# VectorE and ScalarE take over GpSimd's products in a hybrid decoder block, and the S5 response copies are queued later

## The chip, the cores and the metric

One core of one Trainium2 chip runs one launch of the kernel. The metric is device time in microseconds (us) of that core, the median of several executions. Engines are named as the profile names them: PE is TensorE (PEld its weight loads), DVE is VectorE, ACT is ScalarE, POOL is GpSimd, SP is the sync engine, whose queue issues the DMAs (q in a name, as in SPq, is an engine's own queue).

## The reference

One decoder layer for 1024 tokens of width 1024 in float32: a mixer of four gated delta-rule heads beside 32 groups of a complex diagonal state space (S5), then attention to 256 memory tokens, then a SwiGLU, and a last RMSNorm. Cut to what the change touches:

```
q, k, v = silu(causal_conv4(rmsnorm(h) @ w_in))          # 4 heads of 128
g  = -exp(a_log) * softplus(a + dt_bias); beta = sigmoid(b)
o  = gated_delta_rule(l2norm(q), l2norm(k), v, g, beta)  # in chunks
o  = o * rsqrt(mean(o*o) + EPS) * norm_g * silu(z)
x_t = ab * x_{t-1} + bb u_t   (complex)                  # S5, 64 states a group
y  = gelu(Re(C x_t) + D u_t)
y  = y * sigmoid(y @ w_glu + b_glu)
h += concat(o, y) @ w_out
h += cross_attn(rmsnorm(h), rmsnorm(mem)) @ w_xo
h += (silu(n(h) @ w_gate) * (n(h) @ w_up)) @ w_down      # n: rmsnorm
out = rmsnorm(h) * norm_final_g
```

## The kernel before, in words

Every matrix product is made of three matmuls: each operand is split into a high part (ScalarE's copy, L62) and a low part (a subtraction, L63, on VectorE or GpSimd as the caller says), and `mm3` (L79 to L81) adds high x high, low x high and high x low in PSUM. The activations are kept transposed, 128 features by 512 tokens a tile.

The stages follow each other: input norm; S5 set-up, whose four rounds of `s5_pre` leave each group's response in DRAM (TD), from which `s5_toeplitz` copies the tile TT, eight DMAs of 256 KB each from DRAM to DRAM; the gates (`gates`, L525 to L560: decay g, its running sums gc and gr, beta); the memory's norm (`mem_prep`, L804 to L826); four heads, each with its input products, a convolution (L489 to L492), `dn_a` (from L566, which reads gr back through DRAM, gD, into the broadcast tile d_Qg, and takes from it the chunk decays dn_al and d_kdc), `dn_v` and `dn_b`; then, interleaved, the recurrence over chunks (`dn_seq`, `dn_tail`), S5 (`s5_in`, `s5_out`) and the memory's key and value products; `glu`; the out-projection; attention; the SwiGLU's first half; the down products; and `final`.

`s5_out` (L378 to L418) makes, for each pair of groups, complex products of real parts: for real and imaginary part a first product z1 on VectorE (L392, L405), a second product z2 (L393 and L406 on GpSimd, names s_m), their sum or difference (L394, L409), and between the two halves a scan along the tokens (L398, s_S). There are 8 calls with 2 products of each kind in each half, so 32 second products. `dn_tail` (L780 to L800) takes a chunk's output po from PSUM, sums its squares on ScalarE (L791), makes an rsqrt of 11 small VectorE operations (L85 to L89, d_ro), multiplies po by it (L795, VectorE) and by the gate sz (L796, GpSimd), and lets TensorE transpose (L799).

The down products run in five blocks of four activation tiles. `down_acts` loads the block's eight 128x512 tiles, makes differences of them (L1255) and splits them; `down_weights` splits four pairs of weight tiles a block, one of each pair on VectorE (128x1024, whi and wlo from wraw) and one on GpSimd (128x768, from wb); `down_products` adds seven PSUM results a row tile to hT or Q (L1325, VectorE). The last tiles of the SwiGLU's first half are summed at L1197 (VectorE) and multiplied at L1204 (GpSimd) just ahead of it.

PSUM pools: pm has three banks (name mm), p5 one (name aux; the convolutions, the gates and the memory norm use it), p6 one; `final` runs with pa's five.

The order of instructions on each engine isn't the program's: a scheduler in the framework, which simulates a timeline, sets it when the kernel is built; a wait on an engine's queue holds up everything behind it. `issue_after` makes an instruction come no sooner in that order than the one named.

## Time and profile before

| | us |
|---|---|
| median of 3 runs | 1603.62 (1600.15 to 1607.66) |
| profiled execution, its own time | 1605.2 |
| its span | 1603.2 |
| PE busy | 1457.7 (91%) |
| VectorE busy | 1188.9 (74%) |
| GpSimd busy | 655.9 (41%) |
| ScalarE busy | 634.7 (40%) |

The mean granted TensorE clock is 0.958 of full speed. The span is what the trace covers; the profiled execution's own time is 2.0 us longer. A row of a timeline reads: start, duration, engine, line, operation, output and inputs, and in brackets how long the engine stood idle before it and what released it. A row with "x4" is four instructions in a run. A row of a stretch gives the stretch, its length, busy time and instructions (x) of PE, PEld, DVE, ACT and POOL, the granted clock, the share of DMA time and GB/s.

### The profile page before, as it was taken

How to read it: one execution, taken by the hardware profiler on the slowest of the kernel's cores; microseconds unless marked ns; L12 is line 12 of the kernel's file. 1: busy time of each engine (PE TensorE's matmuls, PEld its weight loads, DVE VectorE, ACT ScalarE, POOL GpSimd, SP SyncE). 2: the span in 40 equal slices, each digit the busy share in tenths (PEclk: the TensorE clock that was granted, in tenths of full speed). 3: DMA queues.
4: the chain of work that ended last, by engine and by line, in shares of the span. 5: the costliest groups of instructions: out<-in, count | busy, mean ns of one | idle time of the engine just before them, and what ended most of it. 6: DMA issues, size and time to landing. Idle time of an engine off the chain costs nothing.

```text
span 1603.2 us, 20926 instructions
## 1 busy us (share of the span) xinstructions
PE 1457.7 (91%) x7326; PEld 1218.8 (76%) x7326; DVE 1188.9 (74%) x2164; ACT 634.7 (40%) x1137; POOL 655.9 (41%) x475
## 2 busy tenths in 40 slices
PE   6887699996978788999999999999999998999985
PEld 4787488886877576878888788888888886777864
DVE  8969489886699797775546697666666668899886
ACT  5222353452544563454443442333333334533322
POOL 6175234324552416620010443333333347766544
PEclk9999899997989988999999999999999999999997
DMA  7256454548688152245524414444444357444302
GB/s 224 80 164 199 134 133 124 140 119 293 213 291 265 47 197 105 79 131 171 171 92 165 144 33 145 149 142 139 145 137 137 112 168 251 149 146 150 126 10 105
DMA packets 146616, 237.49 MB, mean 148 GB/s; under 512 B 12464, under 2 KB 79440, under 8 KB 143952
## 3 DMA queue, kind: packets, MB, share of 16 engines
q1 hardware_dynamic: 146512, 236.17, 45.7%
q8 instruction: 57, 0.93, 0.2%
q14 instruction: 47, 0.39, 0.1%
HBM read 169.69 MB, written 68.53 MB: 149 GB/s over the span
## 4 chain that ended last, share of the span: by engine, by line
PE 53%; DVE 24%; DMA 9%; issue 5%; ACT 4%; POOL 3%; SPq 1%; DVEq 0%; POOLq 0%; ACTq 0%
PE aux L81 9%; PE aux L79 9%; PE aux L80 9%; PE mm L81 8%; PE mm L79 8%; PE mm L80 8%; DVE aux L491 2%; DVE wlo L63 1%; DVE d_R L675 1%; DMA s_wb<-in_s5bT 1%; DVE s_S L398 1%; POOL wlo L63 1%; DVE hT L1380 1%; DMA d_R<-LD 1%; DMA wraw<-in_w_xk 1%
## 5 line engine op out<-in xcount | busy, mean ns | idle before, releaser
L62 ACT ACTIVATE whi<-wraw 128x1024 fp32r<-128x1024 f32 (+2 forms) x152 | 139.7, 922 | 202.3 <-PE mm L80 67.3
L79 PE MATMUL mm<-AH,whi 128*128 128x512 f32 x448 | 178.4, 399 | 1.4 <-DVE hT L1325 1.4
L81 PE MATMUL mm<-AH,wlo 128*128 128x512 f32 x432 | 170.9, 396 | 0.0
L80 PE MATMUL mm<-AL,whi 128*128 128x512 f32 x408 | 161.3, 396 | 0.0
L150 POOL TENSOR_TENSOR acc<-acc,sq 128x512 f32<-128x512 f32 (+1 forms) x41 | 53.1, 1295 | 212.9 <-ACT sq L149 212.1
L63 DVE TENSOR_TENSOR wlo<-wraw,whi 128x1024 fp32r<-128x1024 f32 (+1 forms) x76 | 97.9, 1290 | 33.2 <-ACT whi L62 33.1
L1204 POOL TENSOR_TENSOR sg<-sg,ca 128x512 f32<-128x512 f32 x40 | 58.2, 1456 | 144.1 <-DVE sg L1197 92.7
L63 POOL TENSOR_TENSOR wlo<-wraw,whi 128x1024 fp32r<-128x1024 f32 x28 | 67.8, 2422 | 115.8 <-ACT whi L62 98.8
L79 PEld LDWEIGHTS mm<-AH,whi 128*128 128x128 f32 x448 | 84.6, 189 | 20.9 <-DVE hT L1325 2.9
L81 PEld LDWEIGHTS mm<-AH,wlo 128*128 128x128 f32 x432 | 81.5, 189 | 18.3 <-issue 0.4
L80 PEld LDWEIGHTS mm<-AL,whi 128*128 128x128 f32 x408 | 77.1, 189 | 16.6
L80 PE MATMUL aux<-AL,whi 128*128 128x512 f32 x216 | 85.0, 393 | 0.7 <-POOL AL L63 0.7
L79 PE MATMUL aux<-AH,whi 128*128 128x512 f32 x176 | 69.7, 396 | 0.0
L62 ACT ACTIVATE wlo<-graw 128x512 fp32r<-128x512 f32 x62 | 38.8, 626 | 62.7 <-PE aux L81 53.1
L81 PE MATMUL aux<-AH,wlo 128*128 128x512 f32 x160 | 63.4, 396 | 0.0
L491 DVE SCALAR_TENSOR_TENSOR aux<-pre,convw,aux 128x512 f32<-128x512 f32 x72 | 54.1, 751 | 8.3 <-ACT aux L489 7.5
L1202 ACT ACTIVATE ca<-ca 128x512 f32<-128x512 f32 x40 | 25.3, 633 | 83.5 <-DVE ca L1197 83.0
L63 POOL TENSOR_TENSOR wlo<-wb,whi 128x768 fp32r<-128x768 f32 x19 | 39.8, 2094 | 42.3 <-ACT whi L62 42.3
L81 PE MATMUL aux<-AH,whi 128*128 128x512 f32 x136 | 53.4, 392 | 0.0
L80 PEld LDWEIGHTS aux<-AL,whi 128*128 128x128 f32 x216 | 40.6, 188 | 10.6 <-POOL AL L63 1.4
L63 DVE TENSOR_TENSOR wlo<-graw,wlo 128x512 fp32r<-128x512 f32 x40 | 46.0, 1150 | 2.2 <-ACT wlo L62 2.2
L79 PE MATMUL aux<-AH,wlo 128*128 128x512 f32 x120 | 47.3, 394 | 0.0
(713 smaller groups left out, 4678.2 us busy)
## 6 DMA issues: line engine op xcount, KB each, us to landing
graw<-in_w_up SPq DMA_DIRECT2D x22, 512.0 KB
acc<-in_w_down SPq DMA_DIRECT2D x42, 256.0 KB
actD<-sg SPq DMA_DIRECT2D x40, 256.0 KB
WD<-acc SPq DMA_DIRECT2D x40, 256.0 KB
wraw<-in_w_in SPq DMA_DIRECT2D x16, 512.0 KB
d_X<-XD SPq DMA_DIRECT2D x8, 1024.0 KB
wraw<-AD SPq DMA_DIRECT2D x16, 512.0 KB
wraw<-VD SPq DMA_DIRECT2D x16, 512.0 KB
```

Of the source, the lines that this page charges most:

```text
L62: self.a.activation(out=hi, in_=src, func=AF.Copy)
L63: return (eng or self.v).tensor_tensor(out=lo, in0=src, in1=hi.bitcast(F32), op=ALU.subtract)
L79: mm(ps, wh, xh, start=first, stop=False)
L80: mm(ps, wh, xl, start=False, stop=False)
L81: mm(ps, wl, xh, start=False, stop=last)
L150: eng.tensor_tensor(out=acc, in0=acc, in1=tmp, op=ALU.add)
L398: v.tensor_tensor_scan(out=Zs[:, k, q], data0=self.m8[:, 2 * b + q:2 * b + q + 1].to_broadcast([P, P]), data1=Z[:, k, q], initial=0.0, op0 ...
L491: v.scalar_tensor_tensor(out=acc, in0=pre[:, 1 + i:1 + i + HT], scalar=cw(i), in1=acc, op0=ALU.mult, op1=ALU.add)
L675: tt(out=R[:, i, :, 0:i], in0=R[:, i, :, 0:i], in1=X[:, :, 0:i], op=ALU.mult)
L1202: A.activation(out=r, in_=r, func=AF.Silu)
L1204: g.tensor_tensor(out=r, in0=r, in1=sg[o], op=ALU.mult)
L1380: self.v.scalar_tensor_tensor(out=dst, in0=dst, scalar=self.gain(4, m), in1=rb, op0=ALU.mult, op1=ALU.mult)
```

## The change

It has eight parts.

1. `s5_out`: the 32 second products are made by VectorE.
2. `gates` and `mem_prep`: their PSUM tiles come from pm (three banks) and no longer from p5 (one).
3. `dn_a`: dn_al and d_kdc are copied by ScalarE instead of VectorE.
4. `dn_tail`: VectorE multiplies po by sz, and four ScalarE copies scale the quarters by ro.
5. `glu`: the sigmoid is written in place in PSUM, and VectorE multiplies from there, eight times, instead of GpSimd.
6. `down_acts`: all splits and differences are VectorE's; ten operations a block of the down products move from GpSimd.
7. `final`: the broadcast row sums are read from PSUM by VectorE; ScalarE's copy of them serves only GpSimd, which multiplies three of the eight row tiles (m = 1, 3, 5) and no longer four.
8. `s5_toeplitz` is called after the first head's `dn_a`, behind that head's load of d_Qg.

```
@@ s5_out (L393, L406)
-            g.tensor_tensor(out=z2, in0=ri, in1=Pv[:, 1 - k], op=ALU.mult)
+            tt(out=z2, in0=ri, in1=Pv[:, 1 - k], op=ALU.mult)
...
-            g.tensor_tensor(out=z2[:, :, N], in0=ri[:, :, N], in1=Zs[:, 1 - k, :, N], op=ALU.mult)
+            tt(out=z2[:, :, N], in0=ri[:, :, N], in1=Zs[:, 1 - k, :, N], op=ALU.mult)
@@ gates, twice (L551, L557); mem_prep alike (L817)
-        ps = self.p5.tile([P, HT], F32, name="aux")
+        ps = self.pm.tile([P, HT], F32, name="mm")
@@ dn_a (L582, L588, L589)
-        self.load(Qg, self.gD.rearrange("(c h) p -> h c p", h=4)[hd:hd + 1].to_broadcast(sh))
+        self.first = self.load(Qg, self.gD.rearrange("(c h) p -> h c p", h=4)[hd:hd + 1].to_broadcast(sh))
...
-        v.tensor_copy(out=al, in_=Qg[:, :, P - 1])
-        v.tensor_copy(out=kdc, in_=E[:, :, P - 1])
+        A.activation(out=al, in_=Qg[:, :, P - 1], func=AF.Copy)
+        A.activation(out=kdc, in_=E[:, :, P - 1], func=AF.Copy)
@@ dn_tail (L795, L796)
-        v.tensor_tensor(out=on, in0=po, in1=ro.unsqueeze(2).to_broadcast(sh), op=ALU.mult)
-        g.tensor_tensor(out=on, in0=on, in1=sz, op=ALU.mult)
+        v.tensor_tensor(out=on, in0=po, in1=sz, op=ALU.mult)
+        for i in range(4):
+            A.activation(out=on[:, i], in_=on[:, i], func=AF.Copy, scale=ro[:, i:i + 1])
@@ glu (L908 to L911)
-                self.a.activation(out=sg, in_=ps, func=AF.Sigmoid, bias=self.bglu[:, m:m + 1])
+                self.a.activation(out=ps, in_=ps, func=AF.Sigmoid, bias=self.bglu[:, m:m + 1])
...
-                self.g.tensor_tensor(out=yy, in0=yy, in1=sg, op=ALU.mult)
+                self.v.tensor_tensor(out=yy, in0=yy, in1=ps, op=ALU.mult)
@@ down_acts (L1233); its put(...) and sub(...) calls on self.g become g
-        v, g = self.v, self.g
+        v = g = self.v
@@ final (L1373 to L1380)
+        ps = self.pa.tile([P, HT], F32, name="aux")
+        self.row_sums(rs, n // P, ps)
         rb = self.tmp.tile([P, HT], F32, name="res", bufs=2)[:, 0:n]
-        self.rowbc(rs, n // P, rb)
+        self.a.activation(out=rb, in_=ps[:, 0:n], func=AF.Copy)
...
-            if m % 2 == 1:
+            if m in (1, 3, 5):
                 self.g.tensor_tensor(out=dst, in0=dst, in1=rb, op=ALU.mult)
+            elif m == 7:
+                self.v.tensor_tensor(out=dst, in0=dst, in1=ps[:, 0:n], op=ALU.mult)
             else:
-                self.v.scalar_tensor_tensor(out=dst, in0=dst, scalar=self.gain(4, m), in1=rb, op0=ALU.mult, op1=ALU.mult)
+                self.v.scalar_tensor_tensor(out=dst, in0=dst, scalar=self.gain(4, m), in1=ps[:, 0:n], op0=ALU.mult, op1=ALU.mult)
@@ the stages
-                self.s5_toeplitz(S)
...
                         B = self.dn_a(hd, q, k, dp, dx)
+                        if hd == 0:
+                            with self.tc.issue_after(self.first.ins):
+                                self.s5_toeplitz(S)
```

Lines below L550 or so move by one in the changed kernel (L595 stays, L821 becomes L822, L1197 becomes L1198, L1255 becomes L1256).

The scheduler orders the instructions anew. On PE, ahead of the first head's k and q norms, the last small sums stood behind nearly all input products (L79 to L81); L552 and L558 are the gates' sums, L120 and L821 the memory norm's column and row sums, L595 the transposes of the first head's tile `it`. Before:

```order
L821 MATMUL aux<-cst,rsm 128x128 x2
L79 MATMUL mm<-AH,whi 128x512
L80 MATMUL mm<-AL,whi 128x512
L81 MATMUL mm<-AH,wlo 128x512
L595 MATMUL da<-cst,it 128x128 x4
```

After, from the last of the S5 set-up's matmuls (L334):

```order
L334 MATMUL aux<-s_G,s_bb 32x128 x7
L552 MATMUL mm<-gt_g,cst 128x32
L558 MATMUL mm<-cst,gt_g 32x128
L120 MATMUL mm<-ones,acc_1642 128x64 x2
L822 MATMUL mm<-cst,rsm 128x128 x2
L79 MATMUL mm<-AH,whi 128x512
```

All four small sums now stand in one run ahead of 96 products, and L595 (eight at once) follows those.

On SP's queue, in the same place; gr is the running sum's row form, gD its copy in DRAM, wraw the weights to come, kD the finished k. Before:

```order
L54 DMA TD<-s_Ks 16x4x128 x2
L54 DMA TT<-TD 512x128
L54 DMA SD<-s_W_1073 128x2x512
L54 DMA TT<-TD 512x128 x7
L54 DMA gD<-gr 32x128
L54 DMA wraw<-in_w_in 128x1024
L54 DMA d_Qg<-gD 128x8x128
```

After:

```order
L54 DMA TD<-s_Ks 16x4x128 x2
L54 DMA gD<-gr 32x128
L54 DMA wraw<-in_w_in 128x1024 x2
L54 DMA SD<-s_W_1073 128x2x512
L54 DMA d_Qg<-gD 128x8x128
L54 DMA TT<-TD 512x128 x8
L54 DMA kD<-it 128x1024
```

The eight TT copies now stand behind gD and d_Qg, and ahead of kD.

On VectorE, at the last sums of the SwiGLU's first half (ca and sg are its results) and the first operands of the down products (AH, AL). Before:

```order
L1197 TENSOR_TENSOR ca<-res,mm 128x512
L1255 TENSOR_TENSOR AH<-AH 128x512
L1197 TENSOR_TENSOR sg<-res,mm 128x512
L1290 TENSOR_TENSOR acc_11296<-acc_11296 128x256
L1255 TENSOR_TENSOR AH<-AH 128x512
L1291 TENSOR_TENSOR acc_11296<-acc_11295,acc_11296 128x256
L1255 TENSOR_TENSOR AH<-AH 128x512
L1292 TENSOR_TENSOR acc_11295<-acc_11296,acc_11295 128x256
L1197 TENSOR_TENSOR ca<-fsg,aux 128x512
L1293 TENSOR_TENSOR acc_11295<-acc_11295 128x256
L1255 TENSOR_TENSOR AH<-AH 128x512 x2
L1197 TENSOR_TENSOR sg<-fsg,aux 128x512
```

After:

```order
L1198 TENSOR_TENSOR ca<-res,mm 128x512
L1256 TENSOR_TENSOR AH<-AH 128x512 x2
L1198 TENSOR_TENSOR sg<-res,mm 128x512
L1291 TENSOR_TENSOR acc_11312<-acc_11312 128x256
L1256 TENSOR_TENSOR AH<-AH 128x512 x2
L1292 TENSOR_TENSOR acc_11312<-acc_11311,acc_11312 128x256
L1198 TENSOR_TENSOR ca<-fsg,aux 128x512
L1256 TENSOR_TENSOR AH<-AH 128x512 x2
L1293 TENSOR_TENSOR acc_11311<-acc_11312,acc_11311 128x256
L63 TENSOR_TENSOR AL<-AH,AL 128x512 x2
L1198 TENSOR_TENSOR sg<-fsg,aux 128x512
```

More differences and two splits of the first down block stand ahead of the last sg.

14 lines of the change are left out of this document (7 added, 7 removed).

## The prediction

> **What bounds the kernel now.** I read the page first, then the busy time of each engine by stage, then the waits and the timeline wherever TensorE stands still. The profiled execution took 1605.2 us, 1603.2 of it span and 2.0 around it; the median of the runs shown, 1603.62, lies 1.6 below it. About 0.5% or 8 us is what a measurement of this kernel can tell from no change.
>
> ```profile
> PE 1457.7 (91%) x7326; PEld 1218.8 (76%) x7326; DVE 1188.9 (74%) x2164; ACT 634.7 (40%) x1137; POOL 655.9 (41%) x475
> ```
>
> TensorE is busy 91% of the span, so nothing that merely relieves VectorE (DVE) or GpSimd (POOL) counts by itself. What counts are the 145 us in which PE is idle. The busy time by stretch shows where they are; columns are PE, PEld, DVE, ACT, POOL, then the granted TensorE clock, the DMA share and GB/s.
>
> ```profile
> 180.00:190.00 10.00, 1.32 (x8) 0.82 (x6) 1.21 (x4) 3.14 (x4) 4.22 (x2) 0.76 0.20 56
> 190.00:200.00 10.00, 4.03 (x14) 3.42 (x15) 9.54 (x19) 6.51 (x10) 4.99 (x4) 0.56 0.15 50
> 370.00:380.00 10.00, 1.85 (x13) 1.69 (x13) 4.34 (x14) 1.80 (x3) 2.01 (x1) 0.65 0.97 303
> 440.00:520.00 80.00, 64.29 (x475) 61.13 (x476) 73.03 (x179) 38.72 (x99) 31.46 (x29) 0.91 0.84 281
> 550.00:560.00 10.00, 1.26 (x5) 0.86 (x5) 6.85 (x13) 1.95 (x3) 2.61 (x2) 0.69 0.23 82
> 1409.00:1448.00 39.00, 38.68 (x167) 31.07 (x166) 37.42 (x45) 15.88 (x23) 25.16 (x14) 1.00 0.46 148
> ```
>
> PE stands still or goes short in the stretch ahead of the first head (180 to 197), at the memory weights (370), in the S5 states (440 to 520) and at the last delta-rule tail (550); two more such places, the start of the down products and the final norm, have their rows below. The change touches all but 370 directly. In the down products themselves (1409) PE is full and VectorE nearly so: 38.68 and 37.42 of 39.
>
> **The change part by part.**
>
> *The gate and memory sums on other PSUM buffers, al and kdc on ScalarE, the TT copies later.* A row of the waits, then VectorE, SP and PE in order of time:
>
> ```profile
> DVE dn_al L588 <- ACT d_Qg L586: 13.7, 1, 13.7
> 158.96 0.35 DVE L550 RECIPROCAL beta<-gt_e 128x32 f32<-128x32 f32 x1
> ...
> 169.47 5.57 SPq L54 DMA_DIRECT2D TT<-TD  x7
> 172.99 0.16 DVE L129 TENSOR_SCALAR rs_ms<-aux 128x2 f32<-128x2 f32 x1 [4.50 <-PE aux L120]
> 174.96 0.16 DVE L89 SCALAR_TENSOR_TENSOR rsm<-rs_w,rsm 128x2 f32<-128x2 f32 x1
> 175.14 0.62 SPq L54 DMA_DIRECT2D gD<-gr  x1
> ...
> 192.97 2.32 DVE L491 SCALAR_TENSOR_TENSOR aux<-pre,convw,aux 128x512 f32<-128x512 f32 x3
> ...
> 195.97 1.12 PE L595 MATMUL da<-cst,it 128*128 128x128 f32 x4 [14.66 <-ACT it L492]
> ```
>
> VectorE waits 13.7 us at L588 for the chain gD, d_Qg, E, Exp, and the convolution (L491) is queued behind it; PE waits 14.7 us for that. In the new order VectorE has no L588, the sums run ahead of the 96 input products and gD leaves before TT. PE then waits earlier, at the memory norm (L822 right behind L120): VectorE is busy with the gates' sigmoid until L550 ends at 159.3, the norm's small operations take 2.1 (172.99 to 175.12), so the last L822 falls near 161.7, and 96 products at 38.68/167 = 0.232 us end near 184. Before, 24 products more were done ahead of L595, which came at 195.97 and took 1.1. With these 24 (5.6 us) and L595's eight now together (2.0), PE has at 191.6 the work that it had at 197.1: -5.5 us. Bounds: -10 (of the 14.7 only the early wait of some 5 is left) to -2 (the early wait grows to 12, when VectorE takes the S5 tables first). The granted clock of 0.56 behind the idle stretch is a part of that loss. A sentence apart: the Trainium skill, "TensorE: Matmul & The Clock Gate", Part 1, has the clock halved after an idle window of about 3.4 us until about 3.4 us of work have passed; by it each long pause closed saves a further estimated 1.7 us, which would make the three PE pauses here, at 181, 549 and 1338, worth 5 us more than I put down; the rows agree that the clock falls.
>
> In the four heads PE is otherwise full; the same L588 waits fall away there, and ScalarE, 40% busy, takes 8 small copies. I put -1 with the memory weights at 370, where DMA is 97% busy and the eight 256 KB TT copies now lie nearer: -4 to +4.
>
> *S5 second products on VectorE.* Min, median and max in ns of the scan, who waits for it, of half of what moves (L406), and the scan at its worst with the GpSimd operation of that moment:
>
> ```profile
> L398 DVE TENSOR_TENSOR_SCAN s_S<-s_m,s_Z x32: 392/411/2587, 385.0 to 492.0; 128x128 f32<-128x128 f32 x32
>   POOL s_m L406: 18.2, 8
> L406 POOL TENSOR_TENSOR s_m<-s_M,s_S x16: 712/762/1253, 387.0 to 493.3; 128x254 f32<-128x254 f32 x16
> 455.05 2.50 DVE L398 TENSOR_TENSOR_SCAN s_S<-s_m,s_Z 128x128 f32<-128x128 f32 x1
> 454.74 2.53 POOL L63 TENSOR_TENSOR wlo<-wraw,whi 128x1024 fp32r<-128x1024 f32 x1
> ```
>
> The same scan takes 0.41 alone and 2.50 when it lies under a GpSimd operation of 2.53. The 32 products cost VectorE 32 x 0.42 = 13.4. They take 32 x 0.76 = 24 us from GpSimd; if VectorE was held in half of it, 12 come back, and the two sides nearly cancel. What remains is handing over: GpSimd waits 18.2 for the scan, eight times, and VectorE in turn for s_m; for these eight round trips I count 0.6 each, which leaves -4 with rounding (13.4 - 12 - 5), since VectorE (73 of 80) is the bound there. Bounds: -10 (half of the 18.2 on the chain) and +4 (only a quarter of the 24 had held VectorE: 13.4 - 6 - 4). A sentence apart: the Trainium skill, "SBUF — State Buffer", section "SBUF: two separate sides", says that of the two engines whoever starts first holds the shared ports for its whole instruction; the 2.50 agrees with it, and by it all 24 could come back, so the term would be an estimated -14.
>
> *End of the delta rule and the GLU.*
>
> ```profile
> 545.30 0.28 ACT L791 ACTIVATE d_R<-po 128x128 f32<-128x128 f32 x1 [3.09 <-PE po L777]
> 552.15 0.69 DVE L795 TENSOR_TENSOR d_R<-po,d_ro 128x512 f32<-128x512 f32 x1
> 552.97 1.59 POOL L796 TENSOR_TENSOR d_R<-d_R,d_L 128x512 f32<-128x512 f32 x1 [1.95 <-issue]
> 554.62 1.11 PE L799 MATMUL po<-cst,d_R 128*128 128x128 f32 x4 [6.15 <-POOL d_R L796]
> 555.86 1.74 SPq L54 DMA_DIRECT2D kst<-memD  x4
> 559.85 0.58 PE L79 MATMUL mm<-kvh,whi 128*128 128x256 f32 x1 [4.12 <-ACT kvh L62]
> ```
>
> From L795 to L799 stand 2.47 us; afterwards four ScalarE scales of a 128x128 quarter stand there (0.28 each by L791, 1.1 together) and the product with sz is off the chain: -1.4. The kst load, which comes when all of this is done, and the K product behind it move along. The GLU's eight products go from 1.3 on GpSimd to 0.68 on VectorE, and the order puts the last tail further ahead of the last GLU products, so that its rsqrt (546.5 to 552.1) runs under TensorE's work: another -2. Sum -3.5, bounds -6 and -1 (the last GLU product becomes the release of kst).
>
> *Down operands on VectorE.* The start:
>
> ```profile
> 1339.91 0.68 DVE L1197 TENSOR_TENSOR sg<-fsg,aux 128x512 f32<-128x512 f32 x1
> 1340.72 2.12 POOL L1204 TENSOR_TENSOR sg<-sg,ca 128x512 f32<-128x512 f32 x1 [3.28 <-issue]
> 1342.88 3.23 ACT L62 ACTIVATE o<-AH 128x512 fp32r<-128x512 f32 x6 [0.85 <-POOL sg L1204]
> 1343.57 0.80 PE L79 MATMUL aux<-o,whi 128*128 128x512 f32 x1 [5.34 <-ACT o L62]
> ```
>
> From the last add to PE's restart run 3.7 us, and the add itself is late because VectorE worked 25 of the 25 us before it under GpSimd's splits. With these on VectorE it has some seven more operations of 0.61 ahead of that add and none of the holding; TensorE's last sums allow the add 2 us sooner, and L1204 at its uncontended length saves up to 0.8: -3, bounds -6 and 0.
>
> In the products of each later block, ten operations of 0.61 to 0.68 come to VectorE's 37.42, and GpSimd keeps four of its 14 (some 8.6 of 25.16 us). Of VectorE's 45 operations 28 add a PSUM bank, at a length that does not move; the second row gives a run of two with SBUF operands and no GpSimd beside it, one start per 0.61:
>
> ```profile
> L1325 DVE TENSOR_TENSOR Q<-Q,aux x48: 672/675/689, 1384.5 to 1545.6; 128x512 f32<-128x512 f32 x48
> ...
> 559.56 1.29 DVE L943 TENSOR_TENSOR sq<-AL 128x512 f32<-128x512 f32 x2
> ```
>
> At that pace the 28 fill 17.1; the other 17, five of them of double size, take 20.3 and alone would take 22 x 0.61 = 13.4. So some 7 us are holding, and two thirds of it go with two thirds of GpSimd's work. VectorE after: 37.4 + 6.1 to 6.8 - 4.7 to 6 = 37.5 to 39.5, against PE's 38.68. I take 0, with bounds of -2 (PE's own gaps, 0.32 a block) and +10 (2 a block) over the five blocks.
>
> *Final norm from PSUM.*
>
> ```profile
> 1572.08 6.92 DVE L1380 SCALAR_TENSOR_TENSOR hT<-hT,gains,res 128x512 f32<-128x512 f32 x4 [1.88 <-ACT res L139]
> 1579.47 0.66 PE L120 MATMUL aux<-ones,acc 128*128 128x64 f32 x2 [4.47 <-DVE hT L1368]
> 1588.90 3.64 DVE L1380 SCALAR_TENSOR_TENSOR hT<-hT,gains,res 128x256 f32<-128x256 f32 x4 [1.22 <-ACT res L139]
> 1596.30 3.64 DVE L1380 SCALAR_TENSOR_TENSOR hT<-hT,gains,res 128x256 f32<-128x256 f32 x4 [1.73 <-ACT res L139]
> 1596.35 3.31 POOL L1378 TENSOR_TENSOR hT<-hT,res 128x256 f32<-128x256 f32 x4 [4.09 <-ACT res L139]
> L491 DVE SCALAR_TENSOR_TENSOR aux<-pre,convw,aux 128x512 f32<-128x512 f32 x72 | 54.1, 751 | 8.3 <-ACT aux L489 7.5
> ```
>
> L491 with a PSUM operand takes 0.75: four of these and one product are 3.7 for 6.92, and start 0.6 sooner: -3.5 on a stretch where PE waits 4.47 for the add queued behind. For 256 columns, five at about 0.41 make 2.05 for 3.64, started 0.6 sooner: -2.2, ahead of the last rsqrt. In the last round the three GpSimd products end it: 3 x 0.83 for 3.31, -0.8. Sum -6.5, bounds -8.5 (all of the 4.47) and -5.
>
> **Sum.** -5.5 - 1 - 4 - 3.5 - 3 + 0 - 6.5 = -23.5: 1605.2 - 23.5 = 1582 us, which is 22 below the median shown. Taking half the distance of the bounds of each term (about 4, 4, 7, 2.5, 3, 6, 1.5) as independent gives a spread of about 12, so 1570 to 1594 for this case alone. Gates, S5 and the last tail together at their lower bounds (-4.5, -6, -2.5) would give 1569.
>
> **The rivals.**
>
> *Middle hidden.* The gates' gain is paid back at L822, S5's by the added products or by the loads (84% DMA from 440 to 520); only the last tail, the down start at -2 and the final norm stay: 1605.2 - 6.5 - 3.5 - 2 = 1593. For it speaks the 0.97 at 370, against it that VectorE, not DMA, is full at 73 of 80. Chance 0.15.
>
> *VectorE bounds the down products.* The upper bound there, +10, with the middle hidden: 1593 + 10 = 1603, no change to be told. It holds if the moved operations stay held as now. Chance 0.11.
>
> *GpSimd starved there: slower.*
>
> ```profile
> 596.99 11.82 POOL L63 TENSOR_TENSOR wlo<-fsg,wlo 128x512 fp32r<-128x512 f32 x1 [4.30 <-ACT wlo L62]
> 608.87 0.80 PE L81 MATMUL aux<-T,wlo 128*128 128x512 f32 x1 [9.50 <-POOL wlo L63]
> ```
>
> While VectorE worked without a gap on SBUF operands, a GpSimd split of 128x512 took 11.82 and PE waited 9.50. If one of the four weight splits left on GpSimd in each of five blocks meets that, five times 9.50 or 47 are lost: 1582 + 47 = 1629. It decides from four such waits on (the 23.5 gained and 8 more). Against it: 17.1 of VectorE's 38 us are PSUM adds, spread between the others, which leave GpSimd room. Chance 0.07. A sentence apart: by the same section of the Trainium skill a GpSimd operation would wait for one VectorE instruction only, which the 11.82 contradicts; I go by the row.
>
> **How the numbers follow.** Forecast 0.67, 1582. 1593 for the 0.15 case counts mostly as faster. Faster by over 8 us: 0.66 + 0.13 = 0.79; within 8 us: 0.01 + 0.02 + 0.11 = 0.14; slower: 0.07. Range: from those three bounds together, 1569, up to 1600, which takes in the hidden middle and some of the third case; about 2 in 10 is left out.
>
> **What would show it.** Right: the wait of PE on it at L595 shrinks below 8 and the convolutions start before 186; L398's maximum and mean fall and S5 has no wait on s_m from GpSimd; L800 follows L795 within 1.5; PE restarts at the down products within 3; the last round of final takes 2 to 2.5. Wrong: a new PE wait at L822 over 12, VectorE over 38.7 of 39 in a down block with PE under 37.5, a split wlo on GpSimd of over 6 us there with PE behind it, or S5's VectorE above 75 of 80 with a later end of the stage.

## The result, and the profile after

The changed kernel takes 1596.88 us in the median (1590.93 to 1600.38), the kernel before, run in turn with it, 1612.34 (1600.15 to 1618.09): 15.5 us less, a ratio of 0.9908 with a 95% interval of 0.989 to 0.9926. It is faster, by two thirds of the 23.5 us forecast. The profiled execution took 1599.34, 1596.4 of it span. The first profile of before (1605.2) was one of its quicker executions; a second one (c_before, below) took 1615.5, and the two of after took 1599.34 and 1598.76 (c_after). So the profiles put the change at 11.8 us where the medians put it at 15.5, and a stage compared by them is uncertain by some us. Where it matters, I give both pairs. Line numbers are those of before up to L796; behind that they are one higher in the changed kernel, and in `final` some more.

The busy time by engine, from the page of after:

```profile
PE 1469.2 (92%) x7326; PEld 1223.8 (77%) x7326; DVE 1184.5 (74%) x2249; ACT 648.0 (41%) x1179; POOL 525.3 (33%) x374
```

PE's idle time fell from 145.5 to 127.2 (span less busy), by 18.3. But its 7326 matmuls were busy 11.5 us longer, with nothing added to them. In the second pair idle time falls by 19.1 (149.9 to 130.8) and the busy time rises by 2.3 only (1463.9 to 1466.2), so most of the 11.5 is not repeated, and it is not shown to be the change's. The same view by stretch, with the columns of the prediction (PE, PEld, DVE, ACT, POOL, clock, DMA share, GB/s):

```profile
160.00:170.00 10.00, 6.70 (x20) 5.52 (x21) 9.18 (x37) 2.76 (x5) 3.85 (x3) 0.56 0.62 210
...
370.00:380.00 10.00, 6.83 (x70) 6.25 (x69) 1.40 (x2) 1.84 (x3) 2.50 (x2) 1.00 0.92 179
380.00:390.00 10.00, 1.21 (x6) 1.24 (x7) 6.38 (x22) 1.06 (x1) 2.34 (x1) 0.52 0.87 265
440.00:520.00 80.00, 64.84 (x492) 61.06 (x490) 63.89 (x184) 45.08 (x117) 13.68 (x10) 0.94 0.78 270
...
1409.00:1448.00 39.00, 39.00 (x169) 31.55 (x168) 39.00 (x56) 15.50 (x22) 8.83 (x4) 1.00 0.46 149
```

The hole ahead of the first head (180 to 197) is gone, as the next rows show, with a shorter one at 160 in its place. The hole at 370 is still there, only ten us later. In the S5 states VectorE fell from 73.03 to 63.89 of 80, though 32 products came to it. In the down products PE and VectorE are both full.

The gates in order of time:

```profile
163.30 1.19 PE L822 MATMUL mm<-cst,rsm 128*128 128x128 f32 x4 [4.40 <-DVE rsm L89]
174.57 2.34 DVE L491 SCALAR_TENSOR_TENSOR aux<-pre,convw,aux 128x512 f32<-128x512 f32 x3
188.55 1.03 PE L595 MATMUL da<-cst,it 128*128 128x128 f32 x8
```

PE waits 4.4 at the memory norm, the convolutions start at 174.6 and no longer at 193, and the eight of L595 are done at 189.6. The 24 products that stood ahead of L595 before are then still to come, less the four of L595 that were: at 0.232 each, some 4.5 us. So PE has at 194 the work that it had at 197.1, 3 us sooner; by the second pair of profiles (L595 at 200.2 and 188.7) it is 7, in the mean 5.

The last head and what follows it, on all engines in order of time, before (L723 makes the last piece of its inverse d_N; L777 is the output product of the recurrence over chunks, here of chunk 0):

```profile
355.96 1.98 DVE L622 TENSOR_REDUCE d_Lc<-d_tmp 128x128 f32<-128x1024 f32 x1 [0.26 <-POOL d_tmp L577]
366.04 1.04 PE L650 MATMUL da<-cst,it 128*128 128x128 f32 x8
367.12 0.87 SPq L54 DMA_DIRECT2D s_W<-SD  x1
374.13 0.28 DVE L670 COPY d_R<-cst 128x128 f32<-128x128 f32 x1 [5.78 <-DMA d_R<-LD]
379.26 2.05 PE L370 MATMUL aux<-s_U,s_W 128*128 128x128 f32 x8 [8.15 <-DMA wraw<-in_w_xk]
401.41 1.23 DVE L679 TENSOR_TENSOR d_N<-d_X,cst 128x1024 f32<-128x1024 f32 x1
426.11 0.59 ACT L723 ACTIVATE d_N<-db 64x512 f32<-64x512 f32 x1 [0.24 <-PE db L722]
435.15 1.06 PE L777 MATMUL po<-d_R,d_X 128*128 128x128 f32 x8
```

And after, to the first product of K:

```profile
365.07 1.92 DVE L622 TENSOR_REDUCE d_Lc<-d_tmp 128x128 f32<-128x1024 f32 x1 [0.71 <-POOL d_tmp L577]
375.48 0.99 PE L650 MATMUL da<-cst,it 128*128 128x128 f32 x7
376.68 3.08 SPq L54 DMA_DIRECT2D s_W<-SD  x1
382.60 0.28 DVE L670 COPY d_R<-cst 128x128 f32<-128x128 f32 x1 [4.87 <-DMA d_R<-LD]
388.79 2.04 PE L370 MATMUL aux<-s_U,s_W 128*128 128x128 f32 x8 [11.96 <-DMA s_U<-uD]
408.69 1.23 DVE L679 TENSOR_TENSOR d_N<-d_X,cst 128x1024 f32<-128x1024 f32 x1
432.50 0.58 ACT L723 ACTIVATE d_N<-db 64x512 f32<-64x512 f32 x1
439.68 1.06 PE L777 MATMUL po<-d_R,d_X 128*128 128x128 f32 x8
558.47 0.60 PE L800 MATMUL po<-cst,d_R 128*128 128x128 f32 x4
559.57 0.68 DVE L912 TENSOR_TENSOR yy<-yy,aux 128x512 f32<-128x512 f32 x1
563.04 0.58 PE L79 MATMUL mm<-kvh,whi 128*128 128x256 f32 x1 [3.97 <-ACT kvh L62]
```

Every row that stands in both lists comes 4 to 10 us later than before, although L595 started 7.4 sooner. S5's first product waits for s_U and the other tiles, which are loaded into memory that L650's input held until then. The K product starts at 563.0 against 559.9 before; in the second pair of profiles at 569.1 against 567.9. So all that was gained up to 190 is gone at 560, and of the S5, tail and GLU terms nothing shows there either. From the K product to the end the time is 1033.4 and 1027.9 us after, 1043.3 and 1045.9 before: 14.0 less in the mean. This is where the change's gain comes from.

The out-projection keeps the stall that the prediction showed of before, on another split and shorter. GpSimd's split, and PE behind it:

```profile
605.14 8.81 POOL L63 TENSOR_TENSOR wlo<-wraw,wlo 128x512 fp32r<-128x512 f32 x1 [4.30 <-ACT wlo L62]
614.00 0.79 PE L81 MATMUL mm<-T,wlo 128*128 128x512 f32 x1 [4.40 <-POOL wlo L63]
```

The start of the down products: the last add, GpSimd's product, and PE's restart.

```profile
1343.62 0.67 DVE L1198 TENSOR_TENSOR sg<-fsg,aux 128x512 f32<-128x512 f32 x1
1344.43 4.27 POOL L1205 TENSOR_TENSOR sg<-sg,ca 128x512 f32<-128x512 f32 x1 [5.56 <-ACT AL L62]
1349.41 0.55 PE L79 MATMUL aux<-o,whi 128*128 128x512 f32 x1 [4.59 <-ACT o L62]
```

The wait of PE is 4.59 where it was 5.34: GpSimd's product, 2.12 before, now takes 4.27, and for the first 3.1 of it VectorE works without a pause.

The final norm, first and last round:

```profile
1572.59 2.72 DVE L1385 SCALAR_TENSOR_TENSOR hT<-hT,gains,aux 128x512 f32<-128x512 f32 x4 [1.88 <-ACT res L1377]
1575.23 0.68 DVE L1383 TENSOR_TENSOR hT<-hT,aux 128x512 f32<-128x512 f32 x1
1590.06 1.66 DVE L1385 SCALAR_TENSOR_TENSOR hT<-hT,gains,aux 128x256 f32<-128x256 f32 x4 [1.73 <-ACT res L1377]
1590.10 2.09 POOL L1381 TENSOR_TENSOR hT<-hT,res 128x256 f32<-128x256 f32 x3 [3.65 <-ACT res L1377]
```

The 6.92 became 3.3, the rounds of 3.64 became 2.1, as forecast. The waits ahead of them, 1.88 and 1.73, did not shorten: VectorE still starts behind ScalarE's copy.

### The profile page after: what moved, and what is told of

Its sections match the earlier page's. It is cut to its first block, busy times and chain, and to the rows that moved or that the text cites. A ratio compares the mean times of both kernels' runs of the same rounds, so it can differ in the third digit from the quotient of the medians.

```text
span 1596.4 us, 20881 instructions
## 1 busy us (share of the span) xinstructions
PE 1469.2 (92%) x7326; PEld 1223.8 (77%) x7326; DVE 1184.5 (74%) x2249; ACT 648.0 (41%) x1179; POOL 525.3 (33%) x374
## 4 chain that ended last, share of the span: by engine, by line
PE 52%; DVE 10%; DMA 5%; POOL 3%; ACT 3%; issue 2%; SPq 0%; POOLq 0%; DVEq 0%; ACTq 0%
PE aux L81 9%; PE aux L80 9%; PE aux L79 9%; PE mm L81 8%; PE mm L80 8%; PE mm L79 8%; DMA memD<-mst 1%; DMA wraw<-in_w_out 1%; POOL wlo L63 1%; DVE whi L63 1%; DVE hT L1338 1%; PE aux L120 1%; PE db L689 0%; DVE hT L1326 0%; DMA hT<-hD 0%
## 5 line engine op out<-in xcount | busy, mean ns | idle before, releaser
L79 PE MATMUL mm<-AH,whi 128*128 128x512 f32 x448 | 181.1, 405 | 0.4 <-DVE hT L1326 0.4
L81 PE MATMUL mm<-AH,wlo 128*128 128x512 f32 x432 | 172.8, 400 | 0.0
L80 PE MATMUL mm<-AL,whi 128*128 128x512 f32 x408 | 163.6, 401 | 0.0
L1205 POOL TENSOR_TENSOR sg<-sg,ca 128x512 f32<-128x512 f32 x40 | 60.2, 1505 | 158.3 <-DVE sg L1198 89.2
L79 PEld LDWEIGHTS mm<-AH,whi 128*128 128x128 f32 x448 | 86.2, 192 | 20.4 <-DVE hT L1326 0.8
L81 PEld LDWEIGHTS mm<-AH,wlo 128*128 128x128 f32 x432 | 82.6, 191 | 18.7
L80 PEld LDWEIGHTS mm<-AL,whi 128*128 128x128 f32 x408 | 78.9, 193 | 17.2
L80 PE MATMUL aux<-AL,whi 128*128 128x512 f32 x216 | 84.9, 393 | 0.0
L79 PE MATMUL aux<-AH,whi 128*128 128x512 f32 x176 | 69.7, 396 | 0.0
L81 PE MATMUL aux<-AH,wlo 128*128 128x512 f32 x160 | 63.5, 397 | 0.0
L81 PE MATMUL aux<-AH,whi 128*128 128x512 f32 x136 | 53.5, 393 | 0.0
L80 PEld LDWEIGHTS aux<-AL,whi 128*128 128x128 f32 x216 | 40.6, 188 | 9.5
L80 PE MATMUL aux<-AL,wlo 128*128 128x512 f32 x120 | 47.3, 394 | 0.0
L79 PE MATMUL aux<-AH,wlo 128*128 128x512 f32 x120 | 47.2, 393 | 0.0
```

Of the source, the lines that this page charges most:

```text
L79: mm(ps, wh, xh, start=first, stop=False)
L80: mm(ps, wh, xl, start=False, stop=False)
L81: mm(ps, wl, xh, start=False, stop=last)
L1205: g.tensor_tensor(out=r, in0=r, in1=sg[o], op=ALU.mult)
```

## The experiments

All are after with one edit, except where said. Ratios are to the kernel before, run in turn on the same chip.

**The kernels themselves again.** c_after is the changed kernel unedited, c_before the kernel before, profiled once more.

> The changed kernel again, unchanged. Theory A (the idle time of TensorE falls as worked out, and TensorE's half-clock stretches, which the new short waits set off, take part of it back): ratio to before 0.991, PE idle in the first 640 us within 4 us of the 97 of the first profile, and the time that busy matmuls lose to the half clock there again over 36 us (31 in before). Rival B (the clock loss of the one profile was chance): the same idle, clock loss near 31, and a profiled time near 1588.

> The kernel before, profiled a second time, to see how far a stage moves between two executions of one order. If the stage sums of the first profile are typical: PE's wait at L595 is again 14 to 15 us, the first L370 starts at 379 to 381, the starved split of the out-projection is there again (10 us or more), and the execution takes 1603 to 1615. If the heads' ten us (L595 to L370) lie in the scatter between executions and not in the change, the first L370 comes at 385 or later here too.

c_after: 1596.69 (1595.32 to 1598.91), ratio 0.991 (0.9883 to 0.9937). PE's idle time up to 640 us is 101.8 where it was 97.3, and the profiled time is not near the 1588 of the rival. But the first theory's clock loss is not shown to be the change's: as said above, PE's busy time rose by 11.5 us in one pair and by 2.3 in the other. c_before: 1615.47, one execution. In it PE waits 14.5 at L595, the first L370 starts at 385.3, 6 us later than in the first profile, and the starved split is there. Of the 10.6 us between the two spans 6.0 have come together by L370 and 8.0 by K. One execution of the same order moves the middle by several us, so a stage counts here only where several kernels agree.

**One part undone.** The late TT copies (u_toep), the down operands (u_down), the second products (u_z2, and z2a_pool with only those of the first half) put back as they were:

```
@@ u_toep: the stages
-                        if hd == 0:
-                            with self.tc.issue_after(self.first.ins):
-                                self.s5_toeplitz(S)
...
+                self.s5_toeplitz(S)
@@ u_down: down_acts
-        v = g = self.v
+        v, g = self.v, self.g
@@ u_z2: s5_out, L393 and L406; z2a_pool: L393 alone
-            tt(out=z2, in0=ri, in1=Pv[:, 1 - k], op=ALU.mult)
+            g.tensor_tensor(out=z2, in0=ri, in1=Pv[:, 1 - k], op=ALU.mult)
```

> The changed kernel with the eight TT copies queued at their old place, ahead of the gates. Theory A: the copies delay the first head's decay chain by some 5 us, but the convolution no longer waits for that chain, so 0 to 3 us slower than the changed kernel, ratio to before 0.991 to 0.993. Rival C (the copies in their new place come in the way of the S5 loads, on which TensorE waits 12.0 and 2.6 us in the changed kernel): 4 us or more faster than the changed kernel, ratio 0.988 or lower, and those two waits below 9 us together.

> The changed kernel with the down operands split and subtracted as before, half on GpSimd. Prediction's term (start of the down products, -3; their steady part 0): 3 us slower than the changed kernel, ratio to before 0.993, the wait of PE at the start of the down products back to about 5.3 from 4.6. From the changed trace alone, 1 to 3 us slower. Rival (VectorE full at 40 of 40 costs time): equal to or faster than the changed kernel.

> The changed kernel with the 32 second products of the S5 states back on GpSimd. Prediction's term (VectorE's added work and its freed holding nearly cancel, handing over is saved): 2 to 6 us slower than the changed kernel, ratio to before 0.992 to 0.995, with waits of GpSimd on the scan of some 18 us back in the trace. Rival (the added VectorE work lengthens the S5 stage and is where the gain went): 3 us or more faster than the changed kernel, ratio 0.989 or lower.

> The changed kernel with only the 16 second products of the first half (L393) back on GpSimd; the other 16 stay on VectorE. In its order on ScalarE the memory products' copies (mst) come as late as in the variant with all 32 back (7 of 16 behind the last S5 output, none in the changed kernel). Theory O (what costs 11 us in the changed kernel is the order: GpSimd, relieved of the products, splits the memory weights sooner, and the 16 memory products crowd into the S5 stage): as fast as with all 32 back, ratio to before 0.983 to 0.986, 8 to 13 us faster than the changed kernel. Rival V (each moved product costs by its own VectorE time): half of it, ratio 0.987 to 0.989.

u_toep: 1596.12, ratio 0.9908 (0.9879 to 0.9937): that part is worth nothing that shows. u_down: 1603.11, ratio 0.9957 (0.9936 to 0.9978): the down operands bring 6.4 us. In its down block the busy times of PE, VectorE and GpSimd are within 0.1 us those of before:

```profile
1409.00:1448.00 39.00, 38.71 (x167) 30.89 (x166) 37.43 (x45) 15.57 (x22) 25.07 (x14) 1.00 0.49 153
```

u_z2: 1585.16 (1582.49 to 1592.28), ratio 0.9842 (0.9812 to 0.9872), the fastest kernel of the study and 11.5 us below after. z2a_pool: 1592.85, ratio 0.989 (0.9864 to 0.9917), at the end of the second theory's range; but it can't be told from after either, and so it does not decide between the two. u_z2 shows that the second products on VectorE cost time in this kernel. The trace says where: K comes at 564.1 in u_z2, no sooner than in after, but the out-projection has no starved split. The three splits of its first pair on GpSimd, which take 1.82, 1.62 and 8.81 in after, take 1.39, 1.62 and 1.60, and the only wait of PE over 1 us between 595 and 640 is this one:

```profile
PE aux L80 <- DVE T L63: 2.9, 1, 2.9
```

z2a_pool has a starved split, of 11.82, and PE waits 9.6 for it.

**The second products alone, and ScalarE's copy of the memory products.** o_z2 is before with the 32 products on VectorE. mst2 gives the tile mst, through which the memory products leave for DRAM, a second buffer, since ACT waits 14.7 us for it in after (5.3 in before); u_z2_mst2 is u_z2 with the same.

```
@@ mst2: mem_proj (L843)
-                t = pool.tile([P, NMEM], F32, name="mst")
+                t = pool.tile([P, NMEM], F32, name="mst", bufs=2)
```

> The kernel before with one part of the change alone: the 32 second products on VectorE. In its order 13 memory copies stand in a row in the middle of the S5 stage and none behind it. Theory O: slower than before by 3 to 10 us, ratio 1.002 to 1.006. The prediction's term (-4): ratio 0.9975. If the loss comes only together with the other parts: 0.998 to 1.001.

> The changed kernel with two buffers instead of one for the memory products' copies on their way to DRAM (mst). Theory O1 (the crowd costs through ScalarE, which waits 14.7 us for the single buffer's store and holds up the S5 copies behind it): these waits under 4 us, 4 to 9 us faster than the changed kernel, ratio 0.985 to 0.988. Rival O2 (it costs through TensorE and DMA, which the memory products fill in the S5 stage and leave empty behind it): waits gone as well, but ratio 0.990 to 0.993, since the scheduler then packs the memory products still closer.

> The changed kernel with the 32 products back on GpSimd and two buffers for the memory copies. Its order packs the memory products as closely into the S5 stage as the changed kernel does. Theory O2: slower than with one buffer, ratio 0.987 to 0.991 against 0.984. Theory O1: no slower, 0.982 to 0.985.

o_z2: 1604.45, ratio 0.9956 (0.9934 to 0.9978), with the median of before at 1611.72. mst2: 1604.07, ratio 0.9961 (0.9944 to 0.9978), 7 us slower than after. u_z2_mst2: 1594.99, ratio 0.9907 (0.9877 to 0.9937), 10 us slower than u_z2. The second products on VectorE are worth 7 us on before, more than the 4 of the prediction, and cost on after, and a second buffer for mst makes both kernels slower, though in mst2 ACT's wait of 14.7 for the first one's store is gone (in u_z2 it was 2.0 already). In o_z2 the out-projection has no starved split; in mst2 and u_z2_mst2 PE waits 9.4 and 12.4 us for one. An edit in S5 is paid for, or rewarded, 100 us further on, by the order that it leaves there.

**That stall taken away.** nostarve makes the eight splits of the first out-projection pair on VectorE:

```
@@ out_pair (L987)
-            self.split(src[n], w[:, 0:4], w[:, 4:8], None, (self.v, self.g)[x % 2])
+            self.split(src[n], w[:, 0:4], w[:, 4:8], None, self.v if mp == 0 else (self.v, self.g)[x % 2])
```

> After, with the eight weight splits of the first out-projection pair all on VectorE, so that no GpSimd split lies there under VectorE's gate products. Theory one (a GpSimd split stretched by VectorE's stream stops PE): PE's wait of 4.4 us on wlo from GpSimd in the out-projection goes, and nothing takes its place: 3 to 6 us faster than after, ratio .987 to .989. Rival (VectorE is then late itself): a wait on VectorE of the same size stands there, ratio .990 to .993.

1588.6 (1585.74 to 1590.05), ratio 0.9847 (0.9829 to 0.9865): 8 us faster than after, more than the wait of 4.4. The split of 8.81 is now this, and PE has no wait over 1.5 there:

```profile
606.99 0.68 DVE L63 TENSOR_TENSOR wlo<-wraw,wlo 128x512 fp32r<-128x512 f32 x1
```

From K to the first row sums of attention it takes 300.6 us (after 307.9 and 304.6); the wait is 4.4 of the difference, and a lower clock can be the rest (0.86 in the mean from 590 to 640 in after, 1.00 here, 0.93 in u_z2, neither of which has such a wait). This shows the stall to be worth some 5.6 us in after (the mean of the two less 300.6).

It accounts for most of what u_z2 gains, too. The first product of the out-projection, in after this one, stands at the same place in every order:

```profile
595.00 0.39 PE L79 MATMUL aux<-AH,whi 128*128 128x512 f32 x1
```

From it to the sums behind the out-projection (L120) nostarve takes 258.3 us and u_z2 257.7, after 266.2 and 263.2: 6.4 and 7.0 less than the mean of after. The spans of after are 10.7 longer in the mean than that of u_z2; the 3.7 that are left lie in three other stretches, none over 2, which is within what two executions of one order differ. The ratios of u_z2 and nostarve, 0.9842 and 0.9847, can't be told apart.

**The gates and the heads.** u_alkdc puts the two small copies back on VectorE, u_psum the sums back on p5's one bank:

```
@@ u_alkdc: dn_a
-        A.activation(out=al, in_=Qg[:, :, P - 1], func=AF.Copy)
-        A.activation(out=kdc, in_=E[:, :, P - 1], func=AF.Copy)
+        v.tensor_copy(out=al, in_=Qg[:, :, P - 1])
+        v.tensor_copy(out=kdc, in_=E[:, :, P - 1])
@@ u_psum: gates (twice), mem_prep
-        ps = self.pm.tile([P, HT], F32, name="mm")
+        ps = self.p5.tile([P, HT], F32, name="aux")
```

> After, with the copies al and kdc of the four heads back on VectorE; PE's order stays nearly as in after, so it is a test of that one part. Theory one (the copies on ScalarE delay the decays and so the heads): L595 to the first L370 loses 6 to 10 us less, ratio to before .985 to .988. Rival (the heads lose by their order, with the convolutions and short waits, and the copies cost nothing): the loss in the heads stays, VectorE waits again for d_Qg at L588, and the ratio is .990 to .994.

> After, with the gates' and memory norm's sums back on the one bank of p5. Theory one (what the gates gain is given back in the heads, because the same loads and the S5 input set when S5 can start): PE waits 12 to 15 us at L595 again, the heads lose some 7 to 10 us less, the first L370 comes within 3 us of where it does in after, and the ratio is .989 to .993 as for after. Rival (the two places are independent): PE waits at L595 again and the heads keep their loss, ratio .994 to .997; or the heads lose nothing because they lost by another part, ratio below .989.

u_alkdc: 1594.19, ratio 0.9885 (0.9866 to 0.9905), not to be told from after, and between the two forecasts; the trace decides for the rival, since the first L370 still comes at 391.0, after a wait of 11.5. u_psum: 1593.18 (1585.07 to 1598.89), ratio 0.9878 (0.9853 to 0.9904), no slower than after, as the first theory has it, though PE waits at L595 again and the first head starts 9 us later (L595 comes at 197.7; in u_alkdc at 189.7, in u_toep at 190.2):

```profile
PE da L595 <- ACT it L492: 12.7, 1, 12.7
```

So it is the sums on three banks that close the hole ahead of the first head, and neither the copies nor the place of TT. The first L370 comes at 379.6, 9 us sooner than in after, K at 567.3, between the two executions of after (563.0 and 569.1), and the first product of the out-projection at 595.3 (after 595.0 and 600.8). So the sums gain at 190, and by 595 nothing of it is to be seen: what undoes them lies between. The total does not price them alone, since u_psum has no starved split (see below).

**S5 brought forward.** In the traces so far the first L370 follows the end of the last head's L650 by 10 to 14 us: s_W, s_U, s_M and s_T are loaded into the memory that these transposes free. s5_early puts the last head's convolution of v behind its d_Lc, which moves L650 forward and nothing ahead of the last head; early_nostarve adds the edit of nostarve.

```
@@ s5_early: in_tile (L490)
-            for i in (1, 2, 3):
-                v.scalar_tensor_tensor(out=acc, in0=pre[:, 1 + i:1 + i + HT], scalar=cw(i), in1=acc, op0=ALU.mult, op1=ALU.add)
+            with self.tc.issue_after(self.lc.ins) if n == 11 else nullcontext():
+                for i in (1, 2, 3):
+                    v.scalar_tensor_tensor(out=acc, in0=pre[:, 1 + i:1 + i + HT], scalar=cw(i), in1=acc, op0=ALU.mult, op1=ALU.add)
@@ dn_a (L622)
-        v.tensor_reduce(out=Lc, in_=tmp.rearrange("p c (b j) -> p c j b", b=8), axis=AX.X, op=ALU.add)
+        self.lc = v.tensor_reduce(out=Lc, in_=tmp.rearrange("p c (b j) -> p c j b", b=8), axis=AX.X, op=ALU.add)
```

> After, with the last head's convolution of v put behind that head's reduction for d_Lc on VectorE, so that the transposes of v (L650) end earlier on PE, as they do in before; all that stands ahead of the last head is unmoved. Theory one (the gates' gain is lost because L650 comes late and S5's first tiles lie in the memory that it frees): L650 ends 6 to 9 us sooner, the first S5 product still follows it by 11 to 14 us, and so starts at 380 to 384; of this 3 to 6 us reach the K product, ratio .986 to .989. Rival (the S5 stretch is bound elsewhere, by VectorE or its loads): the first S5 product starts sooner, the K product does not, ratio .990 to .993.

> s5_early and nostarve together (the first out-projection pair's splits on VectorE). If the two losses are separate, they add: 8 to 12 us faster than after, ratio .980 to .983. If the first is not worth anything, as nostarve alone: .984 to .987.

s5_early: 1591.31 (1589.19 to 1594.1), ratio 0.9879 (0.9862 to 0.9895). early_nostarve: 1591.58, ratio 0.9873 (0.985 to 0.9895). The rows of s5_early, all engines in order of time:

```profile
371.18 0.60 PE L650 MATMUL da<-cst,it 128*128 128x128 f32 x4
...
380.73 2.04 PE L370 MATMUL aux<-s_U,s_W 128*128 128x128 f32 x8 [4.86 <-DMA s_W<-SD]
...
432.60 0.59 ACT L723 ACTIVATE d_N<-db 64x512 f32<-64x512 f32 x1 [0.71 <-PE db L722]
571.21 0.68 DVE L912 TENSOR_TENSOR yy<-yy,aux 128x512 f32<-128x512 f32 x1
```

S5 starts 8 us sooner, as expected, and nothing comes of it that shows: L723 ends where it did in after, to 0.1 us, K comes at 565.1, and the first product of the out-projection at 593.5. The ratio lies where the first theory put it, but not by its path: that S5's late start loses the gain is not borne out, and the rival's reading stands. The 5 us of s5_early against after lie behind K, where its order has no starved split, and so early_nostarve has nothing to add.

**The serial chain.** The rows show another path: d_Lc goes through DRAM to d_R (17 us from L622 to L670), fifteen small steps of VectorE follow (L673 to L676, each a product and a sum), then the inverse to L723, then eight chunks one behind the other. In after the fifteen steps take from 382.6 to 407, S5's operations being ordered between them. chain_first puts every s5_out behind L679, chain_early does so in s5_early.

```
@@ dn_b (L679): self.n0 = tt(...); the stages
-                    self.s5_out(b, sb, *s)
+                    with self.tc.issue_after(self.n0.ins):
+                        self.s5_out(b, sb, *s)
```

> After, with every s5_out put behind the last head's d_N (L679) in the order, so that its fifteen small steps are not interleaved with S5 on VectorE. Theory one (the chain of the last head and the recurrence sets the end of this part): L670 to L679 takes 7 to 10 us and not 26, the last head's inverse (L723) ends 10 to 16 us sooner, the first L777 comes at 425 to 431 and the K product 8 to 16 us sooner; ratio .982 to .986. Rival (S5 itself, which now starts its products later, sets the end): L723 comes sooner and the K product does not, or comes later; ratio .990 to .995.

> The same on s5_early, where d_Lc of the last head comes some 6 us sooner and S5's first product 8 us sooner. Theory one: L723 ends 4 to 8 us sooner than in chain_first, at 408 to 418, and the K product 12 to 22 us sooner than in after, unless the S5 products then end last; ratio .977 to .984. Rival as there: no gain over s5_early, ratio .987 or more.

chain_first: 1599.28 (1595.34 to 1604.22), ratio 0.9935 (0.991 to 0.9961). chain_early: 1598.43 (1591.25 to 1602.12), ratio 0.9917 (0.9888 to 0.9946). In chain_first:

```profile
393.43 1.23 DVE L679 TENSOR_TENSOR d_N<-d_X,cst 128x1024 f32<-128x1024 f32 x1
425.28 0.58 ACT L723 ACTIVATE d_N<-db 64x512 f32<-64x512 f32 x1
430.62 1.06 PE L777 MATMUL po<-d_R,d_X 128*128 128x128 f32 x8
578.18 0.68 DVE L912 TENSOR_TENSOR yy<-yy,aux 128x512 f32<-128x512 f32 x1
```

The chain is quicker at every row: L679 by 15 us, L777 by 9, the last chunk's L777 at 534 and not 548. K comes at 558.7, 4 us sooner than in the first execution of after and not 8 to 16. But K is no clean mark in this order: as in u_z2, u_psum and s5_early, K products stand ahead of the last GLU product, which comes at 578.2 where it came at 559.6. The out-projection needs both sides, and its first product is the better mark. It starts at 590.7 and 598.8 us in the two executions of before, at 595.0 and 600.8 in those of after, at 593.1 in chain_first and 594.4 in chain_early. So a shorter chain does not move it by more than two executions of one order differ. In after the two sides end within 1.1 us of each other (the last L800 at 558.5, the last L912 at 559.6), they share VectorE and PE, and here one is relieved at the other's cost. That this trade is what holds the mark where it is, is argued and not shown.

What makes chain_first and chain_early slower than s5_early lies behind the mark, 7 to 8 us of it between the mark and L120. There is the stall of the out-projection, which neither forecast had: PE waits 9.4 and 9.0 us for a GpSimd split there. In chain_first it is this one:

```profile
593.65 12.47 POOL L63 TENSOR_TENSOR wlo<-wraw,wlo 128x512 fp32r<-128x512 f32 x1 [43.20 <-ACT wlo L62]
```

So chain_first's ratio lies in the rival's range, but not because S5 sets the end.

**Two more terms of the sum.** u_final puts the final norm back, u_dng the tail's and the GLU's products (parts 7, and 4 with 5, of the change, undone line by line as in its diff).

> After, with the final norm as in before (row sums copied to SBUF for both engines, GpSimd on four row tiles). The prediction's term was 6.5 us, the traces' last stretch shows 9 to 10, two or three of them a higher clock. If the stretch's difference is this part's: 8 to 11 us slower than after, ratio .996 to .998. Rival (the term as predicted, and the rest came from the order ahead): 5 to 7 us slower, ratio .994 to .9955.

> After, with the end of the delta-rule tail and the GLU's product back as in before (ro by VectorE, sz and the GLU product by GpSimd). The prediction's term was 3.5 us (1 to 6). If it is right: from L795 to L799 stand again 2.3 to 2.6 us, and it is 2 to 5 us slower than after, ratio .992 to .994. Rival (the last GLU product and kst hide it): within 1 us of after, ratio .990 to .9915.

u_final: 1604.62, ratio 0.9956 (0.9942 to 0.9969), 7.9 above u_dng, which ran beside it and equals after; this lies between the two forecasts, at the upper end of the prediction's bounds. Its first round has the old length:

```profile
1574.64 6.91 DVE L1381 SCALAR_TENSOR_TENSOR hT<-hT,gains,res 128x512 f32<-128x512 f32 x4 [2.80 <-ACT res L139]
```

u_dng: 1596.7 (1596.04 to 1597.54), ratio 0.9911 (0.9898 to 0.9925): nothing. From its last L795 (554.25) to L799 (556.72) stand 2.47 us as in before, K comes at 562.15, and that is 0.9 sooner than in after.

**The same stall in every kernel.** Most of the orders have the starved split, and it blurs the comparison of their times. PE's wait for it is 4.4 to 5.3 us in after, u_toep, u_alkdc, u_down and u_final; it is 9.0 to 12.4 in before, z2a_pool, mst2, u_z2_mst2, u_dng, chain_first and chain_early; and there is none in u_z2, o_z2, nostarve, u_psum, s5_early and early_nostarve. From the first product of the out-projection to L120 the first group takes 265 us in the mean, the second 268, the third 260. Only nostarve and early_nostarve were written to be without it; the others owe it to the order that the scheduler made. So the total of a kernel with one part undone holds that part and a change in this stall of several us. Two readings suffer by it. u_psum is no slower than after, but against nostarve, which ran beside it and has no such split either, it is 4.6 us slower; the intervals (0.9853 to 0.9904, 0.9829 to 0.9865) overlap, and at the first product of the out-projection the traces show no difference (595.3 and 596.0), so what the gates' sums are worth in the total stays open. And u_dng equals after although its wait is 9.6 and not 4.4, so its 0 is uncertain by that much.

## Why the prediction was right or wrong, point by point

The prediction had the sign and a range that holds the time; its sum was 8 us too large, and the time of 1582 was counted from 1605.2, 7 us below the median of the paired runs of before. That the sum came so near is in part luck: the terms up to K, -14, came to nothing that shows, and those behind K, -9.5, to some -14.

**The step that failed: the terms up to K (gates -5.5, heads -1, S5 -4, tail -3.5) were added to the sum, above all "at 191.6 the work that it had at 197.1: -5.5 us", as if PE's clock ran on from each pause to the end of the kernel.** For the gates the step is right where it was made (5 us in the mean, with a wait of 4.4 at L822 for the estimated 5). What was wrong was to carry it on. Instead of -14 up to K the two pairs of profiles show +3.2 and +1.2; the medians, whose difference is 15.5, would leave -1.5 for this part beside the 14.0 behind K. The rival "middle hidden" is nearest to what happened, by a mechanism that it did not name: it blamed L822, the added products and the loads. The experiments show that neither the start of the heads (u_psum) nor that of S5 (s5_early) nor the fifteen steps (chain_first) moves the first product of the out-projection, which needs both the recurrence and the GLU, by more than two executions of one order differ (593.1 to 595.3, against 595.0 and 600.8). What holds that point is not shown. I had read busy shares and the largest waits, and had not followed which work each of the two sides of the middle still had in front of it. Why the last head falls back by 9 us in the new order (d_Lc at 365.1, with the first head 7.4 ahead) is the scheduler's order of VectorE there: L622 stood ahead of the last convolution of v before and stands behind it now. s5_early, which reverses that, brings L622 to 359.3 and so shows the order to be the reason for most of that row; for the end of the part no effect shows. The prediction also read PE's wait of 14.7 as that for VectorE at L588. In u_alkdc VectorE waits for d_Qg again, 13.0 us in the four heads, and L595 still comes at 189.7; in u_psum VectorE has no L588, and PE waits 12.7. So the sums' bank decides over that wait, and not the copies.

**S5, -4.** The premise, "VectorE (73 of 80) is the bound there", was wrong, though the engine's own account came out better than forecast. Two of VectorE's S5 groups before, and the same after with the two new ones (count, us in total, mean ns, idle before):

```profile
L409 DVE TENSOR_TENSOR s_X<-s_m,s_m 64x254 f32<-64x254 f32 x32 | 23.5, 734 | 2.7 <-POOL s_m L406 1.7 <-PE aux L415 0.4
L398 DVE TENSOR_TENSOR_SCAN s_S<-s_m,s_Z 128x128 f32<-128x128 f32 x32 | 18.1, 604 | 0.1
```

```profile
L409 DVE TENSOR_TENSOR s_X<-s_m,s_m 64x254 f32<-64x254 f32 x32 | 15.4, 480 | 0.5
L398 DVE TENSOR_TENSOR_SCAN s_S<-s_m,s_Z 128x128 f32<-128x128 f32 x32 | 13.1, 464 | 0.0
L393 DVE TENSOR_TENSOR s_m<-s_M,s_P 128x256 f32<-128x256 f32 x16 | 6.7, 419 | 0.0
L406 DVE TENSOR_TENSOR s_m<-s_M,s_S 128x254 f32<-128x254 f32 x16 | 6.6, 413 | 0.0
```

These two groups give back 13.1 us, as much as the 13.3 that the products cost; with L392, L394 and L405 it is 17.5, and 20.5 in the second pair. VectorE has 9 us more room between 440 and 520 and the stage ends no sooner. The Trainium skill, "SBUF — State Buffer", section "SBUF: two separate sides", by which more of the holding would come back than my half (12 of 24), is borne out for the engine; the time is not. (With the terms of my own sum, 13.4 - 24 - 5, that case gives -15.6 and not the -14 that I wrote.) Worse, u_z2 shows the part to cost 11.5 us in this kernel, not by VectorE's time but by the order that it leaves: 7.0 of the 10.7 between the spans lie in the out-projection, where nostarve gains 6.4 by taking the stall away, and no other stretch differs by over 2. Why the scheduler's order has the split with these products stays open; on before, the same products leave an order without it, and o_z2 is 7 us faster.

**Heads and memory weights, -1.** L370 waits 12.0 where it waited 8.15, and starts 9.5 later in the first pair and 6.8 in the second (392.1 against 385.3): outside the bounds of -4 to +4 as a place, though at the first product of the out-projection no such loss is left. u_alkdc shows that the small copies are not the reason.

**Tail and GLU, -3.5.** Not seen: 0 (u_dng, with the doubt said above), and at K and at the first product of the out-projection (595.8) nothing either. I had priced the 2.47 from L795 to L799 as if PE waited there last. In after the last L795 is at 554.53 and L800 at 558.47, since GLU products are ordered between; "within 1.5" was wrong too.

**Down products, -3 and 0.** Undersized: u_down measures 6.4. The restart within 3 did not come, 4.59 remains, because L1205 met the starvation that I had feared for the weight splits: from the last add to the restart run 5.8 us and no longer 3.7. The gain is elsewhere: in before PE waited in the first block also at L80 for a POOL split (0.72) and at L79 for a VectorE add (1.72), and stood 0.32 in each later block; in the two profiles of after one wait of 0.4 and 0.6 is left of these. VectorE is full (39.00 of 39), as in my upper case, and PE too: the point from which it would have cost was met exactly and not passed. "GpSimd starved in the down products" did not occur.

**Final norm, -6.5.** Right in mechanism and undersized: 7.9. The lengths were as forecast and the earlier start of 0.6 did not come; PE's wait of 4.47 is 1.27 now, and the rest can be a higher clock, which is 0.76 over the last 53 us of before and 0.84 over the last 44 of after (0.77 and 0.86 in the second pair):

```profile
1550.00:1603.00 53.00, 30.30 (x177) 27.71 (x175) 33.89 (x71) 17.26 (x39) 27.54 (x27) 0.76 0.23 79
```

```profile
1552.00:1596.00 44.00, 26.41 (x178) 23.79 (x176) 27.59 (x75) 17.62 (x39) 22.57 (x24) 0.84 0.27 96
```

The Trainium skill, "TensorE: Matmul & The Clock Gate", Part 1, had such a gain for long pauses closed; the trace agrees here. Over the whole kernel no gain in clock shows: the mean is 0.956 after and 0.958 before in the first pair, 0.958 and 0.954 in the second.

The forecast's terms by the runs: about 0 up to K (+2.2 by the mean of the two pairs, -1.5 by the medians) and -14.0 behind it, for which the 6.4 of u_down and the 7.9 of u_final account.

## What to carry to other kernels

A pause of the busiest engine is worth its length only if the work behind it sets an end; where two serial strands later meet, as the recurrence and S5 do here, price a gain at the point where they meet and not where the pause is. Where a scheduler orders the program anew, measure each part undone as well as added: here one of eight parts cost 11.5 us where the two best brought 14.3, for the most part through a stall 100 us away. And before a total is put down to the part that was edited, see whether such a stall came or went with it: here it did in most of the kernels. Look also for operations that end late beside a VectorE without gaps, since their length is not their own.

The two versions whose intervals lie wholly below that of after are u_z2 (ratio 0.9842) and nostarve (0.9847).
